# A hybrid decoder block on one core: 28 of its 64 input blocks moved into a Strassen stage, and its attention summed by parts

## The chip, the core and the metric

The kernel runs on one core of a Trainium2 chip as one launch. The metric is device time in microseconds from start to end of the launch, the median over several runs. Work is spread over five engines that run their own instruction lists in order and wait for each other through semaphores: TensorE (PE: matrix products and transpositions, results in PSUM), VectorE (DVE), ScalarE (ACT), GpSimd (POOL) and SyncE (SP: it issues most transfers). A profile is one execution traced by the hardware; rows name an engine, a line of the kernel, and tiles as `out<-in`. "PEld" is PE's load of the stationary operand, which overlaps the products.

## The reference

One decoder layer over 1024 positions of width 1024, with 16 learned tokens put in front (1040 positions in all). All arithmetic is in float32.

```python
h = concat([meta, x])                       # (1040, 1024)
xn = rms_norm(h, g_pre_mix)
b_c, c_c, h_c, q, k, v, g_conv, g_attn = split(xn @ w_in)   # eight parts, 1024 wide each
y_conv = b_c * causal_dwconv(c_c * h_c, conv_w_mix)         # 3 taps
o = stick_breaking_attention(q, k, v)                       # 16 heads of 64
merged = sigmoid(g_conv + b0) * (y_conv @ w_proj_conv) \
       + sigmoid(g_attn + b1) * (o @ w_proj_attn)
h = h + rms_norm(merged @ w_out, g_post_mix)
u, g = split(rms_norm(h, g_pre_ffn) @ w_up_gate)            # 2816 wide each
h = h + rms_norm((gelu(causal_dwconv(u, conv_w_ffn)) * g) @ w_down, g_post_ffn)
return h[16:]
```

The attention has no softmax. With z = q·k/8, f = sigmoid(-z) and S(t,s) the product of f(t,j) over all j with s <= j < t (and S = 1 from s = t on), the weight of key s for query t is A(t,s) = sigmoid(z(t,s)) · S(t,s+1), and zero from s = t on.

## The kernel before

Every float32 product is made of three products of rounded operands ("float32r"): each operand is split into a high part (a cast on ACT) and a low part (a subtraction); high·high, high·low and low·high are summed in PSUM. The helper `split` (lines 64 to 66) does it: line 65 is the ACT cast, line 66 the subtraction, on DVE or POOL by its last argument. So rows with L65 and L66 come from many places, and their tiles tell which.

The activations stand transposed, features on the 128 partitions and positions along the free axis: `xnT` holds the normalised input as 2 (high, low) x 8 feature blocks x 1040 positions. The 8192 columns of `w_in` are 64 blocks of 128. `Dense` (lines 81 to 158) works them off as a list of items; an item is one block: its weights are loaded (512 KB), split (line 110 on ACT, line 113 in four pieces on POOL), and multiplied with `xnT` in three column chunks of 342 to 356 positions, 24 matmuls each (lines 129 to 131): 72 matmuls per block. One `step()` is three matmuls. After a chunk the item's own `evac` takes the sums out of PSUM: for a q block two ACT casts, two DVE casts and two DVE subtractions (lines 229 to 231), for a k block an ACT cast and a DVE subtraction per head (242, 243), for a gate a sigmoid on ACT (304), for the convolution's three blocks a copy (278), a product on DVE (282), three taps (202 to 204) and another product (289).

Eight head pairs follow each other. The list holds, per pair, the v, q and k blocks of the next pair, three convolution blocks and one gate; the last pair has four gates, and five gates are left for the time behind the attention. The first three items are made while the input is still being normalised (`start_items`, `x_block`, lines 418 to 472).

The attention of a head is cut in nine query blocks of 114, in three units of three. `stage1` (lines 316 to 356) makes, per query block, z in chunks (lines 330, 331), f and sigmoid(z) on ACT (332, 333), and, one chunk later, S by a scan on DVE (340), then the product of sigmoid(z) with S shifted by one on POOL (346) and a triangular mask on POOL (348). The tile `fl` holds f and then S; `be` holds sigmoid(z) and then A. `stage2` (lines 358 to 398) transposes A by PE into PSUM tiles `tp` of two buffers (377), splits them (`ah` by ACT line 65, `al` by DVE line 66), and multiplies them with the values (367, 368); a product is issued two key blocks after its transpositions. The last two steps (394, 395) add the halves and write `ot`.

The loop at lines 506 to 536 merges three streams by written costs: stage 1 leads stage 2 by at least 2500 cost units, by at most two units of three blocks, and dense steps are dealt out so that a pair's share of the list ends with the pair's stage 1. The framework then places each engine's instructions; the order stands fixed in the built program.

Behind the attention come the two projections (items `pc` and `pa`), the output projection, and the feed-forward part. Its up-projection already uses Strassen's scheme in Winograd's form (`prep_pair`, `products`, lines 816 to 892): a pair of 128-column blocks is multiplied by seven half-size products instead of eight, each 4 x 3 matmuls on 256 to 512 columns. Weight combinations (`A11`, `S1`, ... tiles `a_op`) are split with the low part on POOL; token combinations (`T1` to `T4`) are made by DVE; three partial sums are copied out of PSUM by ACT (`snap`) and added at the end by DVE (918, 930). For an "u" pair each set of seven products is run twice, on 258 and on 256 columns; for a gate pair once on 512.

## Time and profile before

| | |
|---|---|
| median of 3 runs | 2027.19 us (2023.95 to 2030.04) |
| profiled execution, its own time | 2019.99 us |
| its span, first to last instruction | 2018.2 us |
| PE busy | 1968.4 us, 98% of the span |
| DVE, ACT, POOL busy | 1006.3, 853.3, 1022.7 us |
| mean granted TensorE clock | 0.993 |

How to read it: shares of busy time are means over stages. A row of a group gives busy microseconds, mean nanoseconds of one instruction, and the idle time of the engine in front of it with what ended it. PE's matmuls overlap, so the time of one row is longer than the distance from one start to the next; the distance is what counts. The input stage runs from 0 to about 67 us, the attention with its dense filling to about 925 us, the rest of the mixer to about 1300 us, the feed-forward part to the end.

### The profile page before, as it was taken

To read this page: it belongs to the slowest core of one execution; us is meant where nothing else is said; L and a number is where in the kernel's file an instruction comes from. 1 tells how busy PE (TensorE), PEld (TensorE's weight loads), DVE (VectorE), ACT (ScalarE), POOL (GpSimd) and SP (SyncE) were. 2 spreads that over 40 slices of the span, in tenths; PEclk is the share of its full clock that TensorE was granted. 3 is DMA by queue.
4 is the path that set the end of the run, shared out by engine and by line. 5 is a ranking of instruction groups with operands and counts; after the bars stand their busy time and mean duration, and the time that the engine had idled before them with its cause. 6 is when DMAs were issued, how large, how long until landed. Compare 5 with 4: busy or idle time off the path is not lost.

```text
span 2018.2 us, 30990 instructions
## 1 busy us (share of the span) xinstructions
PE 1968.4 (98%) x12228; PEld 1857.0 (92%) x12228; DVE 1006.3 (50%) x1545; ACT 853.3 (42%) x1771; POOL 1022.7 (51%) x1062
## 2 busy tenths in 40 slices
...
GB/s 137 43 63 43 53 32 64 43 53 43 42 53 43 58 39 62 32 64 73 189 221 156 188 214 114 97 31 126 63 84 67 102 66 82 92 174 111 84 84 136
DMA packets 56174, 177.58 MB, mean 88 GB/s; under 512 B 12872, under 2 KB 12872, under 8 KB 56028
## 3 DMA queue, kind: packets, MB, share of 16 engines
...
## 4 chain that ended last, share of the span: by engine, by line
PE 87%; DVE 7%; ACT 2%; DMA 2%; POOL 1%; issue 1%; ACTq 0%; DVEq 0%; SPq 0%; POOLq 0%
PE mm L129 14%; PE mm L130 14%; PE mm L131 14%; PE st L863 7%; PE st L867 7%; PE st L865 7%; PE tp L377 3%; PE st L1157 3%; PE st L1155 3%; PE st L1156 3%; PE av L368 2%; PE av L367 2%; PE z L331 2%; PE z L330 2%; PE po L706 1%; PE po L708 1%
## 5 line engine op out<-in xcount | busy, mean ns | idle before, releaser
L129 PE MATMUL mm<-xnT,whi 128*128 128x342 f32 (+2 forms) x1536 | 505.5, 329 | 0.3 <-ACT xnT L65 0.2
L130 PE MATMUL mm<-xnT,whi 128*128 128x342 f32 (+2 forms) x1536 | 494.0, 322 | 0.5 <-DVE xnT L66 0.5
L131 PE MATMUL mm<-xnT,wlo 128*128 128x342 f32 (+2 forms) x1536 | 492.3, 320 | 0.0
L346 POOL TENSOR_TENSOR be<-be,fl 114x271 f32<-114x271 f32 (+14 forms) x288 | 206.0, 736 | 310.3 <-DVE fl L340 301.6
L113 POOL TENSOR_TENSOR wlo<-raw,whi 128x256 fp32r<-128x256 f32 x320 | 254.8, 828 | 208.2 <-ACT whi L110 207.3
L130 PEld LDWEIGHTS mm<-xnT,whi 128*128 128x128 f32 x1536 | 291.0, 189 | 2.1 <-DVE xnT L66 1.0
L129 PEld LDWEIGHTS mm<-xnT,whi 128*128 128x128 f32 x1536 | 290.2, 189 | 2.9 <-ACT xnT L65 0.8
L131 PEld LDWEIGHTS mm<-xnT,wlo 128*128 128x128 f32 x1536 | 290.0, 189 | 0.0
L340 DVE TENSOR_TENSOR_SCAN fl<-fl,upper 114x128 f32<-114x128 f32 (+2 forms) x144 | 214.4, 1490 | 112.2 <-ACT fl L332 64.0
L66 POOL TENSOR_TENSOR a_op<-raw,a_op 128x512 fp32r<-128x512 f32 (+1 forms) x136 | 193.7, 1437 | 87.9 <-ACT a_op L65 85.6
L66 DVE TENSOR_TENSOR al<-tp,ah 114x342 fp32r<-114x342 f32 (+3 forms) x288 | 128.3, 452 | 148.8 <-ACT ah L65 147.5
L65 ACT CAST ah<-tp 114x342 fp32r<-114x342 f32 (+3 forms) x288 | 113.0, 398 | 165.3 <-PE tp L377 157.0
L863 PE MATMUL st<-opT,a_op 128*128 128x258 f32 (+2 forms) x528 | 172.3, 326 | 3.2 <-ACT snap L878 1.8
L865 PE MATMUL st<-opT,a_op 128*128 128x258 f32 (+2 forms) x528 | 170.1, 322 | 2.6 <-DVE opT L66 1.7
L867 PE MATMUL st<-opT,a_op 128*128 128x258 f32 (+2 forms) x528 | 170.0, 322 | 0.0
L332 ACT ACTIVATE fl<-z 114x348 f32<-114x348 f32 (+10 forms) x240 | 111.4, 464 | 123.6 <-PE z L331 93.5
L65 ACT CAST a_op<-raw 128x512 fp32r<-128x512 f32 (+1 forms) x136 | 85.1, 634 | 156.0 <-DMA raw<-in_w_up_gate_dram 51.8
L1162 DVE TENSOR_TENSOR acc<-acc,st 128x512 f32<-128x512 f32 x144 | 98.5, 687 | 91.1 <-PE st L1157 91.1
L865 PE MATMUL st<-opB,a_op 128*128 128x512 f32 (+2 forms) x396 | 127.6, 322 | 0.0
L863 PE MATMUL st<-opB,a_op 128*128 128x512 f32 (+2 forms) x396 | 127.6, 322 | 0.0
L867 PE MATMUL st<-opB,a_op 128*128 128x512 f32 (+2 forms) x396 | 127.2, 321 | 0.0
L377 PE MATMUL tp<-ident,be 114*114 114x114 f32 (+1 forms) x720 | 118.5, 262 | 4.1 <-DVE al L66 3.4
(168 smaller groups left out, 4320.5 us busy)
## 6 DMA issues: line engine op xcount, KB each, us to landing
raw<-in_w_in_dram SPq DMA_DIRECT2D x64, 512.0 KB, 3.3
raw<-in_w_up_gate_dram SPq DMA_DIRECT2D x44, 512.0 KB, 3.3
act_d<-owork SPq DMA_DIRECT2D x22, 512.0 KB, 4.3
araw<-act_d SPq DMA_DIRECT2D x22, 512.0 KB
raw<-in_w_down_dram SPq DMA_DIRECT2D x22, 512.0 KB, 3.3
...
```

The lines of the kernel that those rows point to most:

```text
L65: nc.scalar.copy(hi, src)
L66: (lo_engine or nc.vector).tensor_tensor(lo, src, hi.bitcast(F32), op=ALU.subtract)
L113: nc.gpsimd.tensor_tensor(lo[:, c], raw[:, c], hi[:, c].bitcast(F32), op=ALU.subtract)
L129: nc.tensor.matmul(ps, wh, xh, start=(kb == 0), stop=False)
L130: nc.tensor.matmul(ps, wh, xl, start=False, stop=False)
L131: nc.tensor.matmul(ps, wl, xh, start=False, stop=(kb == KB - 1))
L340: nc.vector.tensor_tensor_scan(fl[:, :nk][:, ::-1], fl[:, :nk][:, ::-1], upper[:, NT - nk:][:, ::-1], 1.0, op0=ALU.mult, op1=ALU.max)
L346: nc.gpsimd.tensor_tensor(be[:, a:e], be[:, a:e], fl[:, a + 1:e + 1], op=ALU.mult)
L377: nc.tensor.transpose(tp[:n, QB * j:QB * (j + 1)], blocks[j][0][:, k0:k0 + n], ident[:QB, :QB])
L863: nc.tensor.matmul(ps, wt[:, 0, k], xh, start=start and kb == 0, stop=False, skip_group_check=True)
L865: nc.tensor.matmul(ps, wt[:, 0, k], xl, start=False, stop=False, skip_group_check=True)
L867: nc.tensor.matmul(ps, wt[:, 1, k], xh, start=False, stop=stop and kb == 3, skip_group_check=True)
```

## The change

Three things change together, all ahead of the projections.

**A Strassen stage.** Of the 64 input blocks, 28 leave the list: the convolution's three blocks for seven of its eight column blocks, six attention gates and one convolution gate. They are taken in 14 pairs by the same seven-product scheme as the up-projection, each set of seven products run twice on 260 positions. The two halves of a pair are two 128-column blocks; the two token halves are positions 0 to 519 and 520 to 1039, so that B11, B21 and B22 are read straight from `xnT`, and only T1 to T4 are made, by `token_ops`: per feature block one addition on DVE, one on POOL (high plus low part), four subtractions on DVE and four splits (cast on ACT, low part on DVE). The stage stands behind five plain blocks (the first convolution's three and two gates), during which the token operands are made, and ahead of all attention. The weight combinations (`weight_ops`) are those of lines 829 to 850, with the low part on POOL as there, made for the next pair during a pair. The results go to tiles `su`; what follows on them (product of two blocks, three taps, product with the third, sigmoid, store) is put in a list `todo`, and one entry is taken after each of the first six products of a set.

**A shorter list beside the attention.** The list keeps 36 blocks: the five, 24 of v, q and k, and seven gates, three of them with the last pair and four behind the attention.

**Attention by parts.** Since A(t,s) = S(t,s+1) - S(t,s), the sum of A·v over s is v at the block's last position plus the sum of S(t,s)·(v(s-1) - v(s)). So the values are differenced once per pair (`dv`, DVE), the sigmoid of +z, the products on POOL and the mask go away, stage 2 transposes `fl` itself, and one addition on POOL per pair puts the block-end values back (`VE`). `fl` gets a buffer name per block size (two buffers for the six smaller, one for the three larger), and stage 1 may lead by three units instead of two.

The cut diff (a line of `...` marks what is left out):

```diff
             V[p] = vv
+            ends = VE[p] = heads.tile([P, 9], F32, name="ve", tag="ve", bufs=2)
+            nc.gpsimd.tensor_copy(ends, vt[:, P - 1:NT:QB])
+            dv = work.tile([P, NT], F32, name="dv", tag="wk", bufs=4)
+            nc.vector.tensor_tensor(dv[:, 1:], vt[:, :NT - 1], vt[:, 1:], op=ALU.subtract)
+            nc.scalar.mul(dv[:, 0:1], vt[:, 0:1], -1.0)
...
-                    nc.tensor.transpose(tp[:m, k * P:(k + 1) * P], vt[:, s0:s0 + m], ident)
+                    nc.tensor.transpose(tp[:m, k * P:(k + 1) * P], dv[:, s0:s0 + m], ident)
...
             nk = P + QB * b
             q0 = QB * b
-            fl = work.tile([P, NT], F32, name="fl", tag="fl")[:QB]
-            be = work.tile([P, NT], F32, name="be", tag="be", bufs=6)[:QB]
+            fl = work.tile([P, nk], F32, name="fl", tag=f"fl{b}", bufs=2 if b < 6 else 1)[:QB]
...
                 nc.scalar.activation(fl[:, c0:c0 + n], z, AF.Sigmoid, scale=-0.125)
-                nc.scalar.activation(be[:, c0:c0 + n], z, AF.Sigmoid, scale=0.125)
                 c0 += n
                 if late:
                     late.pop(0)()
                 if c0 < nk:
                     yield n
-            def weights(fl=fl, be=be, nk=nk):
-                nc.vector.tensor_tensor_scan(fl[:, :nk][:, ::-1], fl[:, :nk][:, ::-1],
-                                             upper[:, NT - nk:][:, ::-1], 1.0,
+            def weights(fl=fl, nk=nk):
+                nc.vector.tensor_tensor_scan(fl[:, ::-1], fl[:, ::-1], upper[:, NT - nk:][:, ::-1], 1.0,
                                              op0=ALU.mult, op1=ALU.max)
-                w = -(-(nk - 1) // (-(-nk // 384)))
-                for a in range(0, nk - 1, w):
-                    e = min(a + w, nk - 1)
-                    nc.gpsimd.tensor_tensor(be[:, a:e], be[:, a:e], fl[:, a + 1:e + 1],
-                                            op=ALU.mult)
-                nc.gpsimd.affine_select(out=be[:, nk - QB:nk], in_=be[:, nk - QB:nk],
-                                        pattern=[[-1, QB]], compare_op=ALU.is_gt, fill=0.0,
-                                        base=0, channel_multiplier=1)
 
             late.append(weights)
-            res.append((be, nk))
+            res.append((fl, nk))
...
         if (h, g) == (1, 2):
+            ov = ot[:, :NQ].rearrange("p (b n) -> p b n", n=QB)
+            nc.gpsimd.tensor_tensor(ov, ov, VE[p].unsqueeze(2).to_broadcast([P, 9, QB]), op=ALU.add)
             nc.sync.dma_start(o_d[p * P:(p + 1) * P, :], ot[:, :NQ])
...
-    gate_items = [item_gate(1, ob) for ob in range(8)] + [item_gate(0, ob) for ob in range(8)]
-    n_gate = [1, 1, 1, 1, 1, 1, 1, 4]
-    items, marks = [], []
+    n_gate = [0] * 7 + [3]
+    std_gates = [item_gate(0, ob) for ob in range(1, 8)]
+    gp["p"], gp["n"] = sring, 6
+    items, marks = items_conv(0) + [item_gate(1, 0), item_gate(1, 1)], []
+    n_early = len(items)
     items += [item_v(0), item_q(0), item_k(0)]
     gi = 0
     for p in range(NPAIR):
-        items += items_conv(p)
         for _ in range(n_gate[p]):
-            items.append(gate_items[gi])
+            items.append(std_gates[gi])
             gi += 1
         if p + 1 < NPAIR:
             items += [item_v(p + 1), item_q(p + 1), item_k(p + 1)]
         marks.append(len(items))
-    items += gate_items[gi:]
+    items += std_gates[gi:]
     n_gates = len(items)
-    dense = Dense(ps_mm, items)
+    dense = Dense(ps_mm0, items)
+    dense.stop = n_early
+
+    tops = {}
+    HT = NT // 2
+
+    def token_ops():
+        for kb in range(4):
+            a, b = wk_tile("xa"), wk_tile("xb")
+            nc.vector.tensor_tensor(a, xnT[:, 0, kb].bitcast(F32), xnT[:, 1, kb].bitcast(F32), op=ALU.add)
+            nc.gpsimd.tensor_tensor(b, xnT[:, 0, kb + 4].bitcast(F32), xnT[:, 1, kb + 4].bitcast(F32),
+                                    op=ALU.add)
+            e1, o1, e2, o2 = a[:, :HT], a[:, HT:], b[:, :HT], b[:, HT:]
+            sub(nc.vector, o1, o1, e1)
+            split_top("T1", kb, o1)
+            sub(nc.vector, o1, o2, o1)
+            split_top("T2", kb, o1)
+            sub(nc.vector, e1, o1, e1)
+            split_top("T3", kb, e1)
+            sub(nc.vector, e2, e2, o1)
+            split_top("T4", kb, e2)
+            yield
...
+        start_chunk = start_items(x_block)
+
+    t_ctx = ctx.enter_context(ExitStack())
+    tpool = t_ctx.enter_context(pool("tpool"))
+    for name in ("T1", "T2", "T3", "T4"):
+        tops[name] = tpool.tile([P, 2, 4, HT], F32R, name=f"t{name}")
+    tops_gen = token_ops()
+
+    for i in range(2):
+        next(tops_gen)
+        start_chunk(i, 9)
     dense.i, dense.total = 2, 48
-    dense.until(3)
+
+    RING1 = ["ap", "ap", "ap", "ap", "wlo", "whi", "wlo", "whi"]
...
+    def strassen(a_of, moving, n, bank, snaps, evac):
+        def mm(ps, a, b, start, stop):
+            wt = a_of[a]
+            for kb in range(4):
+                k = slice(kb * P, (kb + 1) * P)
+                xh, xl = moving(b, kb)
+                nc.tensor.matmul(ps, wt[:, 0, k], xh, start=start and kb == 0, stop=False,
+                                 skip_group_check=True)
+                nc.tensor.matmul(ps, wt[:, 0, k], xl, start=False, stop=False,
+                                 skip_group_check=True)
+                nc.tensor.matmul(ps, wt[:, 1, k], xh, start=False, stop=stop and kb == 3,
+                                 skip_group_check=True)
+
+        s = [snaps[k][:, :n] for k in range(3)]
+        b1, b3 = bank()[:, :n], bank()[:, :n]
+        mm(b1, "A11", "B11", True, True)
+        nc.scalar.copy(s[0], b1)
+        yield
+        mm(b3, "S1", "T1", True, True)
+        nc.scalar.copy(s[1], b3)
...
+        mm(b1, "A22", "T4", False, True)
+        evac(1, 0, b1, None)
...
+    def done_ch(cb):
+        if ("c", cb) in mixed and ("h", cb) in mixed:
+            c, y = mixed.pop(("c", cb)), mixed.pop(("h", cb))
+            mixed["y", cb] = y
+            todo.append(lambda: nc.gpsimd.tensor_tensor(c, c, y, op=ALU.mult))
+            todo.append(lambda: None)
+            todo.append(lambda: conv3(y[:, :NQ], c[:, T0 - 2:], NQ, lambda k: w_mix(k, cb)))
+
...
+    def done_gate(which):
+        def done(ob, u):
+            g = u[:, T0:]
+
+            def finish():
+                nc.scalar.activation(g, g, AF.Sigmoid, bias=bias_gate(which, ob))
+                nc.sync.dma_start((gc_d, ga_d)[which][ob * P:(ob + 1) * P, :], g)
+            todo.append(finish)
+        return done
+
...
+    early_blocks = []
+    for cbs in ((1, 2), (3, 4), (5, 6)):
+        for base, done in ((8, done_c), (16, done_h), (0, done_b)):
+            early_blocks += blocks_of(base, done, cbs)
+    early_blocks += blocks_of(8, done_c, [7]) + blocks_of(16, done_h, [7]) + blocks_of(0, done_b, [7])
+    early_blocks += blocks_of(56, done_gate(1), range(2, 8)) + blocks_of(48, done_gate(0), [0])
+    early_pairs = [early_blocks[k:k + 2] for k in range(0, len(early_blocks), 2)]
+
...
+    def prep_early(i):
+        got = early_ops[i] = {}
+        yield from weight_ops(*early_raw.pop(i), got, ring1_tile, tmp_e)
+        load_early(i + 1)
+
...
+    prep = prep_early(0)
+    for k in range(3 * (n_early - 2)):
+        dense.chunk()
+        next(tops_gen, None)
+        if k == 3:
+            load_early(0)
+        elif k > 3:
+            next(prep, None)
+    dense.until(n_early)
+    for _ in prep:
+        pass
+    ps0.close()
...
+    for i in range(len(early_pairs)):
+        last = i + 1 == len(early_pairs)
+        prep = iter(()) if last else prep_early(i + 1)
+        if last:
+            dense.stop = None
+            dense.load(n_early)
+        tiles = [wk_tile("su") for _ in range(2)]
+        for si in range(2):
+            n = HT // 2
+            j0 = si * n
+
+            def moving(name, kb, j0=j0, n=n):
+                return token_op(name, kb, j0, n)
+
+            for k, _ in enumerate(strassen(early_ops[i], moving, n, bank_s, snaps_e,
+                                           early_evac(i, tiles, j0, n))):
+                if (7 * si + k) % 2:
+                    next(prep, None)
+                if k < 6 and todo:
+                    todo.pop(0)()
+                if last and (si, k) == (1, 2):
+                    dense.prep(n_early)
+        for _ in prep:
+            pass
+        early_ops.pop(i)
+    for fn in todo:
+        fn()
+    psS.close()
+    t_ctx.close()
+    early_ctx.close()
...
+    dense.until(n_early + 3)
...
-        if n1 >= len(ends1) or n1 >= n2 + 2:
+        if n1 >= len(ends1) or n1 >= n2 + 3:
```

How it moves instructions, at three places. First PE in the middle of the attention, at the z chunks (`z<-kk`) of a head's last unit, where the blocks of 926 and 1040 keys are made. Before, three dense steps stand between two chunks:

```order
L330 MATMUL z<-kk,qh 114x464
L331 MATMUL z<-kk,ql 114x464
L129 MATMUL mm<-xnT,whi 128x342
L130 MATMUL mm<-xnT,whi 128x342
L131 MATMUL mm<-xnT,wlo 128x342
L129 MATMUL mm<-xnT,whi 128x342
L130 MATMUL mm<-xnT,whi 128x342
L131 MATMUL mm<-xnT,wlo 128x342
L129 MATMUL mm<-xnT,whi 128x342
L130 MATMUL mm<-xnT,whi 128x342
L131 MATMUL mm<-xnT,wlo 128x342
L330 MATMUL z<-kk,qh 114x462
```

In the changed kernel one dense step stands there:

```order
L338 MATMUL z<-kk,qh 114x464
L339 MATMUL z<-kk,ql 114x464
L137 MATMUL mm<-xnT,whi 128x342
L138 MATMUL mm<-xnT,whi 128x342
L139 MATMUL mm<-xnT,wlo 128x342
L338 MATMUL z<-kk,qh 114x462
L339 MATMUL z<-kk,ql 114x462
L137 MATMUL mm<-xnT,whi 128x342
L138 MATMUL mm<-xnT,whi 128x342
L139 MATMUL mm<-xnT,wlo 128x342
L338 MATMUL z<-kk,qh 114x348
L339 MATMUL z<-kk,ql 114x348
```

What moved: two of three dense steps left each gap.

Second DVE at the same depth of the attention: scans (`fl<-fl,upper`) and low parts (`al`). Before, three scans stand ahead of a unit's nine low parts:

```order
L340 SCALAR_TENSOR_TENSOR fl<-fl,upper 114x128
L340 SCALAR_TENSOR_TENSOR fl<-fl,upper 114x242
L340 SCALAR_TENSOR_TENSOR fl<-fl,upper 114x356
L66 TENSOR_TENSOR al<-tp,ah 128x342
L66 TENSOR_TENSOR al<-tp,ah 114x342 x6
L66 TENSOR_TENSOR al<-tp,ah 114x228
L66 TENSOR_TENSOR al<-tp,ah 114x114
L395 TENSOR_TENSOR ot<-av,ot 64x342
L340 SCALAR_TENSOR_TENSOR fl<-fl,upper 114x470
```

In the changed kernel, in a stretch without evacuations:

```order
L347 SCALAR_TENSOR_TENSOR fl<-fl,upper 114x128
L347 SCALAR_TENSOR_TENSOR fl<-fl,upper 114x242
L347 SCALAR_TENSOR_TENSOR fl<-fl,upper 114x356
L347 SCALAR_TENSOR_TENSOR fl<-fl,upper 114x470
L347 SCALAR_TENSOR_TENSOR fl<-fl,upper 114x584
L347 SCALAR_TENSOR_TENSOR fl<-fl,upper 114x698
L66 TENSOR_TENSOR al<-tp,ah 128x342
L66 TENSOR_TENSOR al<-tp,ah 114x342 x6
L66 TENSOR_TENSOR al<-tp,ah 114x228
L66 TENSOR_TENSOR al<-tp,ah 114x114
L393 TENSOR_TENSOR ot<-av,ot 64x342
L347 SCALAR_TENSOR_TENSOR fl<-fl,upper 114x812
```

What moved: six scans in a row stand ahead of the nine low parts, where it was three.

Third PE in the new stage, where the product A11·B11 ends and S1·T1 (`tT_500`) begins. Each triple of lines 560, 562 and 564 stands four times per product; there is nothing between products:

```order
L560 MATMUL st<-xnT,s_op 128x260
L562 MATMUL st<-xnT,s_op 128x260
L564 MATMUL st<-xnT,s_op 128x260
L560 MATMUL st<-tT_500,s_op 128x260
L562 MATMUL st<-tT_500,s_op 128x260
L564 MATMUL st<-tT_500,s_op 128x260
```

What moved: 2352 such rows (14 pairs of 168) stand in one piece ahead of the first z, for 2016 rows of lines 129 to 131 that stood among the attention.

170 lines of the change are left out of this document (140 added, 30 removed).

## The prediction

> **What bounds the kernel now.** I read the page's shares first, then windows of the stages, then PE's waits.
>
> ```profile
> span 2018.2 us, 30990 instructions
> PE 1968.4 (98%) x12228; PEld 1857.0 (92%) x12228; DVE 1006.3 (50%) x1545; ACT 853.3 (42%) x1771; POOL 1022.7 (51%) x1062
> PE 87%; DVE 7%; ACT 2%; DMA 2%; POOL 1%; issue 1%; ACTq 0%; DVEq 0%; SPq 0%; POOLq 0%
> ```
>
> PE is busy for all but 50 us and carries 87% of the chain that ended last. The windows (columns: stretch, its length, busy time and count of PE, PEld, DVE, ACT, POOL, granted clock, DMA) say whether that holds where the change is made:
>
> ```profile
> 0.00:42.00 42.00, 26.19 (x150) 24.16 (x151) 29.89 (x75) 24.80 (x51) 11.18 (x19) 1.00 0.46 165
> 259.10:370.18 111.08, 110.97 (x737) 108.57 (x736) 61.02 (x90) 58.39 (x135) 65.16 (x85) 1.00 0.14 48
> 1050.00:1150.00 100.00, 100.00 (x641) 100.00 (x640) 15.40 (x35) 14.51 (x21) 42.40 (x51) 1.00 0.58 173
> 1450.00:1600.00 150.00, 150.00 (x947) 134.94 (x946) 68.69 (x85) 64.49 (x111) 84.87 (x63) 1.00 0.21 72
> ```
>
> The second is one head pair of the attention, from one scan of 698 keys to the next pair's. PE lacks 0.11 of 111.08 us there; DVE works 61.02 us, 55%. PE is the bound, with much room under it. The first window is the input stage, where PE waits for normalised rows. PE's waits in the whole run:
>
> ```profile
> PE tp L184 <- DVE xn L462: 14.9, 3, 9.1
> PE tp L377 <- DVE al L66: 3.4, 5, 2.1
> ```
>
> The first belongs to the input stage. The second is all that PE loses to the attention's transposition buffers: 3.4 us in 16 heads, 0.21 us a head.
>
> **The matmuls saved.** In the third window only 342-column matmuls run: 641 in 100 us, 0.156 us each. Two plain blocks are 144 of them (a few of 344): 144 x 0.156 = 22.5 us. A pair in the new stage is 7 x 4 x 3 x 2 = 168 matmuls of 260 columns. The nearest row is the up-projection's 258-column matmul; first and last of sixteen in a row:
>
> ```profile
> 1404.25 0.28 PE L863 MATMUL st<-opB,a_op 128*128 128x258 f32 x1
> ...
> 1406.06 0.28 PE L863 MATMUL st<-opT,a_op 128*128 128x258 f32 x1
> ```
>
> Fifteen distances in 1.81 us are 0.1207 us, for 260 columns 0.1216; 168 x 0.1216 = 20.4 us. That saves 2.05 us a pair, **29 us** for 14 pairs. That the scheme saves an eighth of the products is so; the narrower matmul gives part back, since 0.1216 us for 260 columns is dearer per column than 0.156 for 342.
>
> **The new stage's own losses.** Weight combinations, PSUM copies and low parts per pair are those of the up-projection's "u" pairs, and the fourth window shows these with PE full: by the distances above (and 0.233 for 512 columns, as 4.19 us hold 18 of them) 949 matmuls fit in 150 us, and 947 ran.
>
> ```profile
> 1399.84 0.39 PE L867 MATMUL st<-opB,a_op 128*128 128x512 f32 x1
> ...
> 1404.03 0.39 PE L867 MATMUL st<-opT,a_op 128*128 128x512 f32 x1
> ```
>
> The `todo` entries come on top, but DVE and POOL have half of that window free and PE has eight PSUM banks. Between 0.2% and 1% of 286 us is 0.6 to 3 us; I take **+2**.
>
> **Token operands T1 to T4.** They need all of `xnT`, which is complete about here (last transpositions, from the chain):
>
> ```profile
> 39.38 0.88 PE tp L184 x8
> ```
>
> Then PE has 18 steps of the first two items and three whole items, (54 + 216) x 0.156 = 42 us, before the second Strassen product needs T1. DVE has in that time 4 additions of 1040, 16 subtractions and 16 low parts of 520 columns. The rows:
>
> ```profile
> L775 DVE TENSOR_TENSOR xr<-xr 128x1032 f32<-128x1032 f32 (+3 forms) x9 | 16.7, 1856 | 0.1
> L775 DVE TENSOR_TENSOR raw<-raw 128x512 f32<-128x512 f32 x44 | 51.7, 1175 | 107.6 <-POOL a_op L66 106.6
> L775 DVE TENSOR_TENSOR raw<-tmp_s,raw 128x512 f32<-128x512 f32 x21 | 15.6, 744 | 3.2 <-POOL a_op L66 1.2
> L66 DVE TENSOR_TENSOR opT<-xr,opT 128x1032 fp32r<-128x1032 f32 (+3 forms) x8 | 12.6, 1589 | 0.1
> ```
>
> 4 x 1.86 + 16 x (0.74 to 1.18) + 16 x 0.80 = 32 to 39 us. The first convolution's evacuations and taps and the first weight combinations add about 9: 41 to 48 against 42. So PE waits 0 to 7 us at the new stage's door; I take **+3**. What covers this work is the five plain blocks; without them all of it would be seen.
>
> The two widths of like subtractions, 1175 and 744 ns, differ by what POOL does beside them. [...]
>
> **Handover to the attention.** The v block's tile lies where the last gates are stored from; that takes two sigmoids and a store.
>
> ```profile
> act_d<-owork SPq DMA_DIRECT2D x22, 512.0 KB, 4.3
> ```
>
> About 7 us, while three PSUM buffers hold three chunks of 24 x 0.156 = 3.7 us, 11 us. Nothing, or up to 4 if the store queues; **+1**.
>
> **The attention beside a shorter list.** Per pair four of seven blocks go: 4 x 72 x 0.156 = 44.9 us, so PE's 110.97 become 66.0. What leaves the other engines:
>
> ```profile
> L333 ACT ACTIVATE be<-z 114x348 f32<-114x348 f32 (+10 forms) x240 | 110.6, 461 | 0.0
> L346 POOL TENSOR_TENSOR be<-be,fl 114x271 f32<-114x271 f32 (+14 forms) x288 | 206.0, 736 | 310.3 <-DVE fl L340 301.6
> L348 POOL TENSOR_SCALAR_AFFINE_SELECT be<-be 114x114 f32<-114x114 f32 x144 | 113.6, 789 | 10.1
> ```
>
> ACT loses 110.6/8 = 14 us a pair beside the blocks' own work, POOL 40. None of it was on the path, so it gains nothing directly. DVE loses only the convolution's share:
>
> ```profile
> L289 DVE TENSOR_TENSOR yy<-yy,mm 128x342 f32<-128x342 f32 x24 | 12.0, 498 | 1.7 <-PE mm L131 1.7
> L203 DVE SCALAR_TENSOR_TENSOR yy<-cc,par,yy 128x1026 f32<-128x1026 f32 x8 | 10.7, 1339 | 11.8 <-ACT yy L202 11.8
> L204 DVE SCALAR_TENSOR_TENSOR yy<-cc,par,yy 128x1026 f32<-128x1026 f32 x8 | 11.1, 1385 | 0.0
> L282 DVE TENSOR_TENSOR cc<-cc,mm 128x342 f32<-128x342 f32 x16 | 8.2, 512 | 14.5 <-PE mm L131 14.5
> ```
>
> With 4.1 more for eight wider ones of L282, 46/8 = 5.8 us a pair; the differenced values cost one subtraction of 1040, 1.9. DVE: 61.0 - 5.8 + 1.9 = 57.1 of 66.0 us, 86% where it was 55%. PE stays the bound by sums, but DVE runs its list in order, and behind one of its scans wait low parts, behind these the transposition buffers, behind these PE:
>
> ```profile
> L340 DVE TENSOR_TENSOR_SCAN fl<-fl,upper 114x128 f32<-114x128 f32 (+2 forms) x144 | 214.4, 1490 | 112.2 <-ACT fl L332 64.0 <-issue 23.4 <-POOL be L346 21.5
> L340 DVE TENSOR_TENSOR_SCAN fl<-fl,upper 114x128 f32<-114x128 f32 x16 | 7.7, 481 | 16.4 <-ACT fl L332 16.4
> L340 DVE TENSOR_TENSOR_SCAN fl<-fl,upper 114x812 f32<-114x812 f32 x16 | 30.9, 1932 | 23.9 <-issue 14.4 <-ACT fl L332 9.6
> L340 DVE TENSOR_TENSOR_SCAN fl<-fl,upper 114x926 f32<-114x926 f32 x16 | 35.2, 2200 | 11.7 <-issue 9.0 <-ACT fl L332 2.4
> L340 DVE TENSOR_TENSOR_SCAN fl<-fl,upper 114x1040 f32<-114x1040 f32 x16 | 40.1, 2508 | 16.3 <-POOL be L346 9.7 <-ACT fl L332 6.5
> L340 DVE TENSOR_TENSOR_SCAN fl<-fl,upper x141: 424/1375/2853, 68.9 to 924.8; 114x128 f32<-114x128 f32 x16, 114x242 f32<-114x242 f32 x16, 114x356 f32<-114x356 f32 x16, 114x470 f32<-114x470 f32 x16
> ```
>
> Lower bound for PE's wait: today's 0.21 us a head, 3 us in all. Upper: two of the three long scans (mean 2.2 us) uncovered but for two products and a dense step, 5 x 0.156 = 0.8 us: 2 x 1.4 = 2.8 us a head, 45 in all. In between I let the wait grow as share over rest, my estimate: 0.55/0.45 = 1.2 becomes 0.86/0.14 = 6.1, five times, 17 us. If the scans, with POOL's products gone, all took 12% less (424 ns, the least, for a mean of 481 at 128 keys), DVE would have 54 us, 82%, and the factor would be 3.7: 12 us. I take **+14**.
>
> **Sum.** -29 + 2 + 3 + 1 + 14 = -9 us. The profiled execution took 2019.99 us (1.8 beside its span), 7 under the median of 2027.19; I put the difference on the median: **2018 us**. With all losses at their lower ends it is -29 + 1 + 0 + 0 + 3 = -25, 2002; with all at their upper ends -29 + 3 + 7 + 4 + 45 = +30, 2057.
>
> **Rivals.** *All losses hide:* 2002. For it speaks that DVE and PE are each below their sums and that stage 1 may now run three units ahead; against it that only one dense step is left between z chunks.
>
> *DVE's order becomes the bound, slower:* the place is a unit's start in stage 2, where long scans stand ahead of or between low parts. Price 2.8 us a head, 45 in all: -29 + 6 + 45 = +22, 2049. It decides from 1.4 us a head, (29 - 6)/16. For it speaks the 86%; against it that a scan's result is needed a unit later, so DVE may run late for a while.
>
> *The token operands are late:* if DVE and POOL hold each other up beyond the rows above, say 12 us in place of 3, the sum is 0: 2027.
>
> *The change doesn't do what it says:* the stage has 2352 matmuls where 2016 go, so this is excluded; only its size is open.
>
> **How the numbers follow.** Forecast 0.42, its own range 2006 to 2027; all hidden 0.25; DVE's order 0.20; late operands 0.13. 0.3% of the median is 6 us, about what a measurement tells from no change: faster means under 2021, slower over 2033. Faster: 0.29 of the forecast, 0.25, 0.02 = 0.56; same: 0.13 and 0.07 = 0.20; slower: 0.20 and 0.04 = 0.24. The range goes from just under the best sum to just under the slow rival's: 1999 to 2045.
>
> **What would show it.** Right: a new stage of about 288 us with PE full; 67 to 68 us between the scans of 698 keys of two pairs; PE's wait for `al` some 14 us in all; little wait for T1. A pair period of 66 us means all hidden, of 69 or more the slow rival. Wrong altogether it would be if PE's 260-column matmul were not 0.12 us apart, or if a load or a store, not DVE, held PE in the new stage.

## The result and the profile after

| | before | changed |
|---|---|---|
| median, us | 2027.10 (2023.95 to 2030.04) | 2086.39 (2084.05 to 2088.0) |
| ratio | | 1.0288, 95% interval 1.0272 to 1.0305 |
| span of the profiled execution, us | 2018.2 | 2083.5 |
| granted clock, mean | 0.993 | 0.986 |

The change is slower by 2.9%; 0.4% faster was forecast. The page of the changed kernel, its span, shares and chain by engine:

```profile
span 2083.5 us, 31488 instructions
PE 1973.4 (95%) x12564; PEld 1833.2 (88%) x12564; DVE 1110.3 (53%) x1694; ACT 836.4 (40%) x1702; POOL 811.9 (39%) x643
PE 56%; DVE 11%; DMA 7%; ACT 4%; POOL 4%; issue 4%; ACTq 0%; DVEq 0%; SPq 0%; POOLq 0%
```

PE has no less busy time than before (1968.4), although the stage saves 29 us of matmuls, and 110 us of the span without work where it was 50. PE carries 56% of the chain in place of 87%. Windows of the changed kernel (columns as in the prediction: stretch, length, busy time and count of PE, PEld, DVE, ACT, POOL, granted clock, DMA) say where:

```profile
50.00:75.40 25.40, 18.41 (x105) 17.56 (x103) 25.12 (x23) 9.03 (x14) 18.44 (x12) 0.92 0.12 42
75.40:80.00 4.60, 4.58 (x16) 4.58 (x17) 4.60 (x6) 1.90 (x4) 3.37 (x3) 0.50 0.01 4
97.10:409.90 312.80, 293.93 (x2354) 291.68 (x2353) 106.63 (x157) 109.44 (x220) 152.76 (x110) 0.96 0.24 72
609.82:682.73 72.91, 68.57 (x447) 62.86 (x447) 54.48 (x83) 40.16 (x94) 15.28 (x17) 1.00 0.09 30
1069.80:1165.30 95.50, 91.84 (x576) 90.04 (x576) 27.48 (x51) 20.93 (x38) 26.02 (x33) 1.00 0.62 201
1165.30:1260.30 95.00, 92.32 (x578) 91.73 (x577) 15.05 (x40) 18.93 (x33) 56.09 (x62) 0.98 0.69 192
```

In order: the plain blocks of the start (PE idle for 7 of 25 us, then 4.6 us at half clock), the whole new stage, one head pair of attention, and the two projections, which the kernel before did in

```profile
1014.20:1104.30 90.10, 90.10 (x577) 90.10 (x577) 26.56 (x47) 19.38 (x34) 26.40 (x33) 1.00 0.57 189
1104.30:1196.20 91.90, 90.57 (x578) 90.29 (x577) 15.30 (x40) 18.94 (x33) 57.04 (x62) 1.00 0.70 199
```

And PE's waits in the whole run of the changed kernel:

```profile
PE tp L375 <- DVE al L66: 21.4, 31, 1.0
PE st L560 <- ACT snap_e L570: 13.9, 4, 4.1
PE st L560 <- DVE su L666: 4.9, 6, 2.9
PE tp L269 <- DVE vv L66: 4.8, 7, 0.8
PE mm L137 <- DVE yy L298: 4.7, 1, 4.7
PE mm L137 <- DVE gal L876: 2.6, 1, 2.6
PE mm L137 <- DVE gcl L855: 2.6, 4, 0.9
PE z L338 <- ACT fl L340: 2.1, 7, 0.4
PE tp L269 <- DVE dv L262: 2.0, 6, 1.0
```

The last matmul that reads `xnT` (end of the gates) stands at 1069.5 us where it stood at 1014.0: +55.5. The prediction had -9 up to there. The pieces:

- **Start.** The stage begins at 97.1 us. By the prediction's own rows PE could have been there at 39.4 + 0.9 + 42 = 82, but those rows take the last transpositions but one for the last. The last of all, of the last 16 positions, ended at 43.5 us here; 264 of the 360 matmuls of 0.156 us were left then, which gives 84.7. That is +12.
- **New stage.** 312.8 us for what took 14 x 22.5 = 315 us in plain blocks: a gain of 2 instead of 29.
- **Attention with its handover.** What is left: 55.5 - 12.4 + 2 = +45. From the third on a pair takes 72.7 to 72.9 us, not 66.0. Counted from the stage's end at 410.0 us, 31 blocks of 11.23 us and eight pairs without their blocks (66.0 - 3 x 11.23 = 32.3 us each) would be through at 1016.5 us: 53 us are lost. The same rates put the kernel before 7 us too early, and the difference is the +45 again.
- **Behind.** The projections take 95.5 and 95.0 us, where they took 90.1 and 91.9: +8.5. All that follows is within 2 us.

### The profile page after: what moved, and what is told of

Its sections match the earlier page's. It is cut to its first block, busy times and chain, and to the rows that moved or that the text cites. A ratio compares the mean times of both kernels' runs of the same rounds, so it can differ in the third digit from the quotient of the medians.

```text
span 2083.5 us, 31488 instructions
## 1 busy us (share of the span) xinstructions
PE 1973.4 (95%) x12564; PEld 1833.2 (88%) x12564; DVE 1110.3 (53%) x1694; ACT 836.4 (40%) x1702; POOL 811.9 (39%) x643
## 4 chain that ended last, share of the span: by engine, by line
PE 56%; DVE 11%; DMA 7%; ACT 4%; POOL 4%; issue 4%; ACTq 0%; DVEq 0%; SPq 0%; POOLq 0%
PE st L1120 6%; PE st L1122 5%; PE st L1124 5%; PE mm L139 5%; PE mm L138 5%; PE mm L137 5%; PE st L1414 3%; PE st L1412 3%; PE st L1413 3%; DVE fl L347 3%; PE tp L375 3%; PE av L366 2%; DMA xv<-in_x_dram 2%; PE av L365 2%; POOL a_op L66 2%
## 5 line engine op out<-in xcount | busy, mean ns | idle before, releaser
L121 POOL TENSOR_TENSOR wlo<-raw,whi 128x256 fp32r<-128x256 f32 x208 | 177.9, 884 | 315.4 <-ACT whi L118 288.3
L137 PE MATMUL mm<-xnT,whi 128*128 128x342 f32 (+2 forms) x864 | 286.3, 332 | 6.5 <-DVE yy L298 4.7
L138 PE MATMUL mm<-xnT,whi 128*128 128x342 f32 (+2 forms) x864 | 279.9, 324 | 0.9 <-DVE xnT L66 0.9
L139 PE MATMUL mm<-xnT,wlo 128*128 128x342 f32 (+2 forms) x864 | 279.8, 324 | 0.6 <-POOL wlo L121 0.6
L66 POOL TENSOR_TENSOR a_op<-raw,a_op 128x512 fp32r<-128x512 f32 (+1 forms) x136 | 193.7, 1438 | 90.1 <-ACT a_op L65 87.6
L69 DVE TENSOR_TENSOR raw<-raw 128x512 f32<-128x512 f32 x72 | 72.1, 1001 | 209.9 <-POOL a_op L66 106.3
L137 PEld LDWEIGHTS mm<-xnT,whi 128*128 128x128 f32 x864 | 164.9, 191 | 9.1 <-DVE yy L298 5.0
L138 PEld LDWEIGHTS mm<-xnT,whi 128*128 128x128 f32 x864 | 164.9, 191 | 2.6 <-DVE xnT L66 1.4
L139 PEld LDWEIGHTS mm<-xnT,wlo 128*128 128x128 f32 x864 | 164.5, 190 | 0.9 <-POOL wlo L121 0.9
L66 DVE TENSOR_TENSOR al<-tp,ah 114x342 fp32r<-114x342 f32 (+3 forms) x288 | 122.4, 450 | 54.5 <-ACT ah L65 51.8
L65 ACT CAST a_op<-raw 128x512 fp32r<-128x512 f32 (+1 forms) x136 | 85.1, 634 | 159.2 <-DMA raw<-in_w_up_gate_dram 54.5
L560 PE MATMUL st<-tT,s_op 128*128 128x260 f32 x448 | 129.8, 290 | 18.9 <-ACT snap_e L570 13.9
L375 PE MATMUL tp<-ident,fl 114*114 114x114 f32 (+1 forms) x720 | 117.1, 266 | 22.3 <-DVE al L66 21.4
L66 POOL TENSOR_TENSOR s_op<-raw,s_op 128x512 fp32r<-128x512 f32 x84 | 118.7, 1426 | 42.4 <-ACT s_op L65 33.8
L1122 PE MATMUL st<-opB,a_op 128*128 128x512 f32 (+2 forms) x396 | 127.8, 323 | 1.8 <-DVE opB L66 1.8
```

The costliest lines, as they stand in the source:

```text
L65: nc.scalar.copy(hi, src)
L66: (lo_engine or nc.vector).tensor_tensor(lo, src, hi.bitcast(F32), op=ALU.subtract)
L121: nc.gpsimd.tensor_tensor(lo[:, c], raw[:, c], hi[:, c].bitcast(F32), op=ALU.subtract)
L137: nc.tensor.matmul(ps, wh, xh, start=(kb == 0), stop=False)
L138: nc.tensor.matmul(ps, wh, xl, start=False, stop=False)
L139: nc.tensor.matmul(ps, wl, xh, start=False, stop=(kb == KB - 1))
```

## The experiments

Where a run is read by stretch, the pair of attention is measured from one pair's subtraction `dv` to the next's, and the new stage from its first to its last matmul. The diffs show only the lines that matter, and their comments are this text's. "One run" is a single timed execution with its profile. The executions of the kernel before lie between 2017.7 and 2030.0 us, so a few microseconds between the totals of single runs mean nothing; a pair's period mostly repeats within 0.3 us inside a run.

### Each part alone

The first kernel is the kernel before with attention by parts, all else as before (seven equal `fl` buffers):

```diff
-            nc.scalar.activation(be[:, c0:c0 + n], z, AF.Sigmoid, scale=0.125)
-            for a in range(0, nk - 1, w):          # be *= next fl, on GpSimd
+            nc.vector.tensor_tensor(dv[:, 1:], vt[:, :NT - 1], vt[:, 1:], op=ALU.subtract)
-            res.append((be, nk))
+            res.append((fl, nk))
```

> The kernel before with the attention by parts alone; the list of blocks beside the attention is as long as before, fl has seven equal buffers and stage 1 leads by at most two units. Theory (the loss in the attention comes from DVE's order with too little dense work between, not from the sum by parts): a head pair still takes 111 to 112 us, the total is within 8 us of the kernel before, 2019 to 2035. Rival (the sum by parts itself costs: the differenced values are late for the transposition of v, or the one addition on POOL holds the store): 2 us or more a pair, 2043 or more.

Measured: 2039.19 us, ratio 1.0081 (1.0062 to 1.0101); a pair 112.7 us for 111.1 before. From its waits:

```profile
PE tp L184 <- DVE v L73: 16.7, 1, 16.7
PE tp L268 <- DVE dv L261: 3.6, 7, 1.2
PE tp L371 <- DVE vv L66: 3.3, 6, 0.6
```

In between the theory and the rival: the sum by parts costs 1.6 us a pair beside the long list. PE's new waits stand at the value block, whose copy, subtraction and split it reaches too early. The first row lies in the input stage, whose rows have other buffers in this kernel than in the change: PE's first product on `xnT` begins 6 us later than before, and these are not the sum's.

The second is the changed kernel with the old attention (lead of two units):

> The changed kernel with the attention of the kernel before (sigmoid of +z, product and mask on POOL, lead of two units); stage and short list stay. Theory: the short list is what exposes DVE's order, so a pair takes 72 us or more, and with POOL's products beside the scans some us more: total 2080 to 2110. Rival (the sum by parts costs): clearly under the changed kernel, 2060 or less.

Measured: 2187.22 us, ratio 1.0817 (1.078 to 1.0854), a pair 86 to 89 us, PE waiting for `be`, `ah` and `al`. The theory's side, but far beyond its 2110: beside the short list the sum by parts, with the lead of three units that goes with it, is worth 100 us. Neither half of the change alone was faster than the kernel before.

### The start

DVE, POOL and PE in the changed kernel at 66 to 76 us:

```profile
66.74 0.69 DVE L69 TENSOR_TENSOR xb<-xb,xa 128x520 f32<-128x520 f32 x1
72.01 2.93 DVE L69 TENSOR_TENSOR xa<-xa 128x520 f32<-128x520 f32 x1
74.87 0.92 DVE L298 TENSOR_TENSOR yy<-yy,mm 128x342 f32<-128x342 f32 x2
```
```profile
70.97 3.42 POOL L431 TENSOR_TENSOR xb<-xnT 128x1040 f32<-128x1040 f32 x1 [1.78 <-DVE tT L66]
```
```profile
75.42 0.66 PE L137 MATMUL mm<-xnT,whi 128*128 128x342 f32 x1 [4.69 <-DVE yy L298]
```

A subtraction of 520 columns takes 0.69 us, and 2.9 us where POOL's 3.4 us sum of `xnT` runs: it ends 0.55 us after that sum does (three of the sixteen subtractions take as long, and end 0.55 to 0.57 us after such a sum). The plain b block's evacuation (L298) stands behind, and PE waits 4.7 us for it. The granted clock is 0.50 from 74.5 to 81.3 us, so the 6 us of work that follow take 3 us more. Earlier waits of 1.7 us for `whi` and 0.6 for `wlo` have a stretch of 3.4 us at 0.50 with them, from 54.1 us on: 1.7 us more. Together that is 11.7 of the 12.4 us. The kernel before shows the same: 44 of the 65 subtractions of 512 columns in the prediction's two rows of L775 began with no instruction of POOL running and took 0.68 to 0.69 us; the other 21 began while one ran, took 1.30 to 1.79 us, and ended 0.55 us after it.

The experiment puts two more gates into the start (seven plain blocks, 13 pairs) and moves the b block back:

```diff
-    items = items_conv(0) + [item_gate(1, 0), item_gate(1, 1)]
+    items = cv[:2] + [item_gate(1, 0), item_gate(1, 1), cv[2], item_gate(1, 2), item_gate(1, 3)]
-        next(tops_gen, None)
+        if k % 3 == 1:
+            next(tops_gen, None)
```

> The changed kernel, with two more attention gates as plain blocks ahead of the new stage (seven plain blocks, 13 pairs of products instead of 14), the plain b block two places later, and the token operands and weight operands spread over the longer time. By the matmuls alone it costs 22.5 - 20.4 = 2.1 us. Theory: the start loses 12-15 us since VectorE has token operands, taps and the b block's evacuation at once and is busy 10 of 10 us from 60 to 90 us; with 22 us more of plain blocks it is not: the stage begins at 108-112 us instead of 97.1 + 22.5 = 119.6, and the run is at 2076-2082 us. Rival: the start's loss is the weight operands' chain (ScalarE, GpSimd), which is as long whatever stands ahead: the stage begins at 117-121 us and the run is at 2086-2091 us.

Measured (one run): 2072.0 us, below the theory's 2076. The stage begins at 113.9 us, between theory (108 to 112) and rival (117 to 121): 5.7 us before the 119.6, and the wait for `yy` is gone with the half clock behind it. So VectorE's queue is the larger part of the start's +12, 4.7 + 3.0 us. What is left, 6 us, is the waits for `whi` and `wlo` with their half clock (4.0) and 1.0 us for a gate's evacuation at the stage's door; 1 us stays open.

### The new stage

One of three stalls of 4.1 us in the stage, on ACT and POOL of the changed kernel, with windows around it (a fourth of the kind takes 1.7 us):

```profile
211.06 1.16 ACT L203 ACTIVATE su<-su,par 128x1026 f32<-128x1026 f32 x1 [1.48 <-POOL su L606]
214.64 1.15 ACT L203 ACTIVATE su<-su,par 128x1026 f32<-128x1026 f32 x1 [2.42 <-POOL su L606]
215.69 0.35 ACT L570 COPY snap_e<-st 128x260 f32<-128x260 f32 x1
```
```profile
208.60 2.42 POOL L606 TENSOR_TENSOR su<-su 128x1040 f32<-128x1040 f32 x1
212.22 2.38 POOL L606 TENSOR_TENSOR su<-su 128x1040 f32<-128x1040 f32 x1
```
```profile
212.00:216.10 4.10, 0.04 (x1) 0.00 (x1) 3.73 (x2) 1.68 (x4) 2.60 (x2) 0.80 0.41 128
216.10:222.00 5.90, 5.90 (x29) 5.90 (x30) 4.82 (x5) 1.12 (x3) 1.54 (x1) 0.56 0.00 0
222.00:232.00 10.00, 10.00 (x86) 10.00 (x85) 2.66 (x5) 3.37 (x8) 3.57 (x3) 1.00 0.01 2
```

ACT waits 2.42 us for POOL's product c·y, to take the first tap; behind the tap, on the same queue, stands the copy of a PSUM sum to `snap_e`, for which PE waits. After 4.1 us without work PE runs 5.9 us at 0.56 of its clock: 29 matmuls where some 50 would fit. In the stage 18.9 us are idle (312.80 - 293.93) and 293.93 - 14 x 20.4 = 8 us are busy time beyond the sum; the mean clock of 0.96 fits them.

Four experiments took this apart. First the product on DVE:

```diff
-            todo.append(lambda: nc.gpsimd.tensor_tensor(c, c, y, op=ALU.mult))
+            todo.append(lambda: nc.vector.tensor_tensor(c, c, y, op=ALU.mult))
```

> The changed kernel with the product of two convolution blocks in the new stage on DVE instead of POOL. Theory (ACT's tap waits for POOL's product, and the PSUM copy that PE needs stands behind that tap on ACT; each stall of 4 us is followed by a stretch at half the granted clock): the waits for snap_e (13.9 us) go, the stage falls from 313 to 290 to 297 us, total 2065 to 2072. Rival (the stage is short of operands or loads): stage over 308 us, total 2080 or more.

Measured: 2071.61 us, ratio 1.0242 (1.0225 to 1.0259). The total is as expected, the stage is not: 304.5 us, between theory and rival. The waits for `snap_e` are gone, those for `su` rise from 4.9 to 12.8 us. About 5 us of the total came behind attention, in the projections.

Then the taps later:

```diff
-            todo.append(lambda: conv3(y[:, :NQ], c[:, T0 - 2:], NQ, lambda k: w_mix(k, cb)))
+            todo.extend([lambda: None] * 4)      # once both products of a pair are posted
+            for t in taps: todo.extend(conv_steps(*t))   # one tap to a step
```

> The changed kernel, with one thing moved: the two products c*y of a pair of c and h blocks are still GpSimd's, but the three taps of each stand four product steps later, one tap to a step, where the change put all three two steps behind the product. Theory: the new stage loses its time because ScalarE's first tap waits for GpSimd's product with the copy of a PSUM sum to snap_e queued behind it, 4 us each time, after which the granted clock falls: with the taps later the stage falls from 312.8 us to 288-295 us and the run to 2060-2070 us. Rival: the stage is short of VectorE or GpSimd time in the sum over it; then the stalls move to another place and the stage stays above 305 us, the run above 2077 us.

Measured (one run): 2084.13 us, waits for `snap_e` 13.9 us as before. Nothing had moved: in the order as built both first taps stood ahead of the same `snap_e` copy again, for the framework had not kept them where they were written. In the changed kernel's own order, too, the first taps of both blocks stand together: one per product step is how the finishing is written, not how it is issued. With the taps held behind what is written ahead of them (and other edits in the other stretches):

```diff
+        return [lambda: tc.keep_in_program_order(nc.scalar.activation(d, ...)),
+                lambda: tap(1), lambda: tap(0)]          # held in the same way
```

> The changed kernel with three edits, each read in its own stretch. Start: the two further plain gates of the run before. New stage: the taps four steps later, as tried before, but now held in the order in which they are written (before, the scheduler had put them ahead of the copy to snap_e again, so that nothing had moved on ScalarE). Attention: each scan is likewise kept behind what is written ahead of it on VectorE. Theory for the stage (ScalarE's taps stand ahead of the copies while GpSimd's product is late): the waits for snap_e go, and 13 pairs take 268-275 us (20.6-21.2 us each); rival (the sums on VectorE are the bound): above 282 us. Theory for attention (scans standing ahead of al): the pair falls from 72.8 to 69-71 us; rival (the order of the lumps of work on TensorE sets it): 72-73.5 us. Run by the theories 2028-2047 us, by the rivals above 2062 us.

Measured (one run): 2073.39 us. The `snap_e` waits are gone, but 13 pairs take 285.0 us, 21.9 each, the rival's number: the stalls are now `su`, up to 3.4 us. DVE of this kernel:

```profile
245.15 4.18 DVE L623 SCALAR_TENSOR_TENSOR su<-su,par 128x1026 f32<-128x1026 f32 x2
249.25 0.42 DVE L684 TENSOR_TENSOR su<-st,snap_e 128x260 f32<-128x260 f32 x1
```
```profile
249.72 0.39 PE L562 MATMUL st<-tT,s_op 128*128 128x260 f32 x1 [3.40 <-DVE su L684]
```

No single tap or product is the cause, then, but a tight place that each of them can hit. In `strassen` bank b1 is read by `evac(1, 1, b1, ...)` and written again by A22·T4; between stands one product, 12 x 0.12 or about 1.45 us, and the two taps take 4.18. With the taps two steps apart a pair still took 21.6 us (run g3 below). The last experiment widens the place: the halves of a pair's tokens alternate, product by product, each with its own snap buffers, so that three products lie between a sum's reading and its next writing (the expectation counted two).

```diff
-        for si in range(2):
-            for k, _ in enumerate(strassen(...)):
+        halves = [strassen(early_ops[i], moving, n, bank_s, snaps_e[si], ...) for si in range(2)]
+        for j in range(14):
+            next(halves[j % 2])
```

It was run with edits of attention (h1, expectation below). Its 13 pairs, and then for comparison the 13 of the run with the longer start, whose stage was otherwise the change's:

```profile
113.40:381.10 267.70, 262.83 (x2183) 261.61 (x2184) 116.49 (x147) 98.21 (x201) 142.56 (x98) 1.00 0.25 76
```
```profile
113.90:402.70 288.80, 271.18 (x2183) 269.27 (x2184) 102.26 (x147) 99.23 (x201) 139.99 (x98) 0.96 0.23 70
```

(The first is of h2, the same stage again.) 20.6 us a pair for 22.2, clock 1.00 for 0.96, and DVE is no less busy, with taps of up to 3.4 us. That settles the stage: not load, but one product of slack against a queue worked off in order, and the lower clock behind the long stalls. (The order and the second set of snap buffers came together; which of them alone would do, no run tells.)

### Attention

DVE and PE of the changed kernel at one stall:

```profile
621.53 2.31 DVE L347 TENSOR_TENSOR_SCAN fl<-fl,upper 114x1040 f32<-114x1040 f32 x1
623.76 0.91 DVE L66 TENSOR_TENSOR al<-tp,ah 114x342 fp32r<-114x342 f32 x2
```
```profile
623.17 0.32 PE L137 MATMUL mm<-xnT,whi 128*128 128x342 f32 x1
624.31 0.41 PE L375 MATMUL tp<-ident,fl 114*114 114x114 f32 x2 [0.82 <-DVE al L66]
```

A scan stands ahead of `al`, `al` frees a transposition buffer, PE waits for the buffer. 1.14 us lie between two starts that are 0.16 apart when nothing waits; the wait is shown as 0.82, since it counts from the modelled end. Counted by the period, a pair loses 72.8 - 66.0 = 6.8 us, where the rows of waits above (21.4 + 4.8 + 2.1 + 2.0 in 8 pairs) show 3.8.

How much of it are scans? This run leaves out the scan of the first half of each block's keys:

> The changed kernel with the scan left out for the first half of each query block's keys, so the weights of those keys are not the attention's; all else runs. Theory (PE waits because a low part stands behind a scan on DVE): scans are at most half as long, DVE loses about 12 us a pair, a pair falls from 72.8 to 67 to 69 us, total 2045 to 2058. Rival (the round trip PE, ACT, DVE, PE over two transposition buffers sets the pace): a pair stays at 71 us or more, total 2072 or more.

Measured (one run): 2054.67 us, a pair 69.6 to 69.9 us, the wait for `al` 6.0 us in place of 21.4. The total is the theory's, the pair just above it. Scans make 3.1 of the 6.8 us at least. The run can't say whether by their load or by where they stand. Single edits of the changed kernel for the other candidates, first e8, then e4:

```diff
-            dense.defer(1, lambda: tokens(0, 4, P))
+            dense.defer(8, lambda: tokens(0, 4, P))
...
-    ps_mm = psA.enter_context(pool("ps_mm", 3, space=PSUM))
+    ps_mm = psA.enter_context(pool("ps_mm", 2, space=PSUM))
-    ps_tp = psA.enter_context(pool("ps_tp", 2, space=PSUM))
+    ps_tp = psA.enter_context(pool("ps_tp", 3, space=PSUM))
```

> The changed kernel, with the transpositions of a pair's value differences dv put 8, 11 and 14 dense steps behind the end of the value block, where the change put them 1, 2 and 3 steps behind it. Theory: 1.65 us a pair is lost because TensorE's queue reaches these transpositions before ScalarE's copy, VectorE's subtraction and the split are through; later, they cost nothing: the pair falls from 72.8 to 70.8-71.5 us, the run to 2070-2079 us, and the waits of tp for dv and vv go. Rival: VectorE's order as a whole holds TensorE, and a wait that goes there comes back as a wait for al: the pair stays at 72.3-73 us, the run within 5 us of 2086 us.

> The changed kernel, with three PSUM buffers for transpositions and two for the dense blocks, where it has two and three. Theory (VectorE's order): scans of 1.6 to 2.3 us stand ahead of al, and one more buffer of 0.7 us of TensorE's work covers a part of each stall: the pair falls from 72.8 to 70.5-72 us, and the run to 2068-2080 us, unless the dense blocks' evacuation holds TensorE instead. Rival: the two transposition buffers are what set the pace, and VectorE's order does not matter: the pair falls to 66-68 us and the run to 2031-2048 us. Third: the dense blocks need their third buffer more, and the run is above 2090 us.

Measured (one run each): e8 2083.83 us, a pair 71.9 to 73.6; the waits for `dv` and `vv` (6.8 us) are gone, those for `al` are as large as before (14.8 and 7.3 at two places), and pair and run are the rival's. e4 2079.83 us, a pair 71.5: its theory by the numbers, and the wait moved to the product (`av` for `al`, 21.8). Scans held in order (f1, above): 72.6, the rival. With the third buffer in addition:

> The kernel of the run ahead of this one (start, taps and scans held in order) with three PSUM buffers for transpositions and two for dense blocks. By itself the third buffer moved the wait from the transposition to the product and brought 7 us in the run. Theory (what is left is jitter between TensorE and VectorE, which one more buffer evens out): 1-2 us a pair below the run ahead of this, 8-16 us in all. Rival: the wait only moves to the products again, within 0.5 us a pair of the run ahead, or worse for the dense blocks.

Measured (one run): 2075.79 us, a pair 72.0: 0.6 below f1, so nearest the rival. Then the order itself. The rule of stage 1 and 2 writes up to 12 steps of one kind in a row; the next two alternate them:

```diff
-        if n2 < len(ends1) and done1 < min(ends1[n2] + LAG, total1):
-            pick2 = False
+            at = ends1[n2] - u1 * min((ends2[n2] - done2) / u2, 1.0)
+            pick2 = done1 >= min(max(ends1[n2] + 800.0, at + 3200.0), total1)
```

> Start and taps as in the two runs ahead of this. In attention the order is written evenly: the rule that lets the sums of logits run ahead goes by the place within a unit, so that steps of the two halves alternate (one to three at a time), where the change writes lumps of up to 12 steps of one half; scans over 400 keys in two chained pieces; transpositions of dv later. Theory (VectorE has 57 us of work in 66, and only lumps make it late): the pair falls to 67-69 us, the run to 2012-2030 us. Rival (in an even order each scan stands ahead of an al that TensorE is about to want, and there is no stretch without them): the pair stays at 71-74 us, the run at 2045-2070 us.

> The even order of the run ahead of this with three PSUM buffers for transpositions and two for dense blocks. Theory: in the even order the wait for al is short each time, and one more buffer takes most of it: 1-2 us a pair below the run ahead, at 66-68 us a pair, the run at 2005-2022 us. Rival: within 0.5 us a pair of the run ahead.

Measured (one run each): 2087.57 and 2088.17 us, a pair mostly 75.4 and 74 to 76.5. The rivals' side, and worse than they had it: worse than the lumps. The two pieces of each scan stood side by side in the order as built, so that a low part behind them still waited for a whole scan.

Is it the list that is too short, or DVE that is too full? One gate a pair back into the list, at the expense of two pairs of the stage; and 4.4 us a pair off DVE (g1 is the first edit, g3 the second, g2 both):

```diff
-    n_gate = [0] * 7 + [3]
+    n_gate = [1] * 7 + [0]
...
-                nc.vector.tensor_copy(hi[other, c], ps[own])
+                nc.scalar.copy(hi[other, c], ps[own])
-            nc.vector.tensor_tensor(dv[:, 1:], vt[:, :NT - 1], vt[:, 1:], op=ALU.subtract)
+            nc.gpsimd.tensor_tensor(dv[:, 1:], vt[:, :NT - 1], vt[:, 1:], op=ALU.subtract)
```

> Of the 16 gate blocks four are plain ahead of the new stage, one is in it, seven stand in the list beside attention (one to a pair of heads, four blocks a pair instead of three) and four behind it; the new stage has 11 pairs of blocks. The taps are held in order and stand on steps of their own, none behind another. Theory (the list is too short to cover attention's waits): a pair with its gate takes 77.3-79 us (66.0 + 11.25 for the gate, and up to 1.7 of stalls), the run 2017-2030 us. Rival (the stalls are the same whatever the list): 82.5-84 us a pair and the run at 2055-2066 us. New stage: 20.5-21.0 us a pair if VectorE's row of taps was what held it, 21.9 if not.

> The run ahead of this with work taken off VectorE: the copy of q to the other half of the partitions goes to ScalarE (3.1 us a pair), the difference dv to GpSimd (1.3 us), and the transpositions of dv stand 8 to 14 steps later. Theory (list): within 1 us a pair of the run ahead, since one gate covers nearly all. Rival (VectorE's load): 2 us or more a pair below the run ahead.

> The changed kernel's list (no gate beside the first seven pairs), with the start of seven plain blocks, the spread taps, and the same 4.4 us a pair taken off VectorE. Theory (list): the pair falls by 1.7 us or less, to 71-72.7 us, and the run is at 2050-2062 us. Rival (VectorE's load, as in the run with half the scans, where 13 us a pair less load brought 3.1): 69-70.5 us, and the run below 2046 us.

Measured (one run each): g1 2081.61 us, a pair 84.0, which is 72.75 + 11.25: the gate covers nothing, the rival, with a total 15 us above it. Its stage takes 21.5 us a pair, near the 21.9 that was to mean that the row of taps was not it. g2 2084.44 us, a pair 82.9: 1.1 below g1, between theory and rival. g3 2070.94 us, a pair 73.1: neither, for a pair got no shorter at all. So one more block does not help, and 4.4 us less work on DVE brings 1.1 us or nothing. Only beside seven blocks a pair (e1) was the loss down to 1.6 us.

What was left as an explanation was that several limits hold at once: any one taken away, the next holds. The run with all of these edits, and the wide stage:

```diff
+            for j in range(np_):                 # two pieces over 500 keys
+                late.append(lambda j=j, piece=piece: piece(j))   # one to a step, held in order
```

> The changed kernel with: the start of seven plain blocks (13 pairs in the new stage); the two halves of a pair's tokens alternating product by product in the new stage, with a set of snap buffers each; in attention the even order (a step of logits to one or two steps of products), scans of over 500 keys in two pieces that are held in the written order so that al stands between them, three transposition buffers, and the copy of q to the other half of the partitions on ScalarE, dv on GpSimd, its transpositions later. Theory for the new stage (the row behind a PSUM sum is read by VectorE only 1.45 us, one product, before the sum is written again, and any tap of 1.3-2.9 us in front stalls TensorE): with 2.9 us between, 20.4-20.8 us a pair, 265-271 us in all; rival (VectorE's load as such): 279 us or more. Theory for attention (bursts of scans, and a transposition buffer freed only by al, both at once): 66-68 us a pair; rival (even order is worse by itself, as the two runs with it): 72-75.5 us a pair. Run: 1998-2018 us by the theories, where the kernel before takes 2018-2023 us; 2055-2070 us if only the stage's holds.

Measured: 2027.61 us, ratio 1.0027 (1.0015 to 1.0039); the stage 267.7 us, a pair 67.5 to 69.2 us, on the mean 68.5. (This kernel leaves out the last pieces of the last head's scans, some 2 us of DVE's work.) Both by the theories, attention half a microsecond above, and the run 10 us above theirs: the projections still waited. One long stall is left in a pair, 1.97 us between starts; DVE, POOL and PE there:

```profile
571.80 0.82 DVE L66 TENSOR_TENSOR al<-tp,ah 128x342 fp32r<-128x342 f32 x2
572.54 2.63 DVE L354 TENSOR_TENSOR_SCAN fl<-fl,upper 114x406 f32<-114x406 f32 x1
575.10 0.24 DVE L66 TENSOR_TENSOR al<-tp,ah 114x114 fp32r<-114x114 f32 x1
```
```profile
572.40 1.91 POOL L262 TENSOR_TENSOR dv<-vt 128x1039 f32<-128x1039 f32 x1
```
```profile
575.40 0.46 PE L374 MATMUL av<-al,vv 114*128 114x114 f32 x1 [1.81 <-DVE al L66]
```

406 keys take 1.0 us alone; here 2.63, begun 0.14 us after POOL's subtraction and ended 0.9 us after it, as in the start. That subtraction is `dv`, moved to POOL to relieve DVE. The stall also decides between the two lengths of a pair. Of the six pairs with this stall four had the half clock behind it, as in the first row, and two had not:

```profile
575.40:578.40 3.00, 3.00 (x11) 2.94 (x12) 1.54 (x2) 0.90 (x2) 0.98 (x2) 0.50 0.33 90
644.40:647.80 3.40, 3.40 (x25) 3.35 (x26) 2.23 (x4) 2.20 (x6) 0.97 (x2) 1.00 0.41 143
```

The pairs that began with the half clock took 69.0 to 69.2 us, those without 67.5 to 67.6. So in this run an idle stretch of 1.8 us cost some 1.4 us of clock on top in four of six cases.

The next run mends behind attention (six PSUM buffers for dense blocks):

```diff
+    psA.close()
+    dense.ps = psA.enter_context(pool("ps_mm3", 6, space=PSUM))
-            nc.gpsimd.tensor_tensor(ov, ov, VE[p]...)
+            nc.vector.tensor_tensor(ov, ov, VE[p]...)
```

> The run ahead of this (even halves, even order, three transposition buffers, held scan pieces) with: six PSUM buffers for the dense blocks once attention is over, in place of two; the addition of the last values to ot on VectorE instead of GpSimd; transpositions of dv 12 to 20 steps later; and a scan that is always written before the first transposition that reads it (in the run ahead of this the last head's last pieces were left out, some 2 us of VectorE). Theory: waits for gt, gcl and gal behind attention (3.1, 1.6 and 4.7 us) go, attention falls by 0.5-1 us a pair, and the run is at 2005-2016 us, ratio to the kernel before 0.993-0.998. Rival: with the waits for PSUM gone the projections wait for the loads of gates at the same places, and the stall at the scan beside GpSimd stays: 2020-2028 us, ratio 0.999-1.003.

Measured: **2013.92 us, ratio 0.9952 (0.9933 to 0.9971)**, beside 2022.73 of the kernel before: by the theory, and 0.5% faster than the kernel before. PE's waits for `gt`, `gcl` and `gal` in the projections are gone, and these take 90.2 and 91.5 us; the pair stays at 68.2 on the mean, so that part of the expectation failed and the stall beside POOL stays:

```profile
PE 1945.0 (97%) x12540; PEld 1835.2 (91%) x12540; DVE 1111.7 (55%) x1716; ACT 846.4 (42%) x1741; POOL 805.4 (40%) x644
PE av L383 <- DVE al L66: 11.9, 9, 1.8
PE st L578 <- ACT snap_e L594: 2.8, 3, 1.0
```

Last, the same with the lumps back:

> The run ahead of this with the change's own rule for the order of logits and products in attention (lumps of up to 12 steps of one kind), all else as there: three transposition buffers, scan pieces held in order, the copy of q on ScalarE and dv on GpSimd. Theory (bursts of scans are what stalls, and they come of the lumps): the pair goes from 68.2 back to 71 us or more, the run to 2035 us or more. Rival (buffer, pieces and VectorE's load did it, the order matters little): within 1 us a pair of 68.2, and the run at 2010-2022 us.

Measured (one run): 2033.98 us, a pair 70.7. Between the two, nearer to the theory: the lumps cost 2.5 us a pair, and buffer, held scans and DVE's relief together 2.0 (72.7 to 70.7), though singly they brought 1.2, 0.1 and nothing (the scans there were held whole, here in two pieces).

## Why the prediction was wrong, step by step

**Matmuls saved, -29: right.** First and last of 57 matmuls in a row in the changed kernel's stage:

```profile
204.72 0.28 PE L560 MATMUL st<-tT,s_op 128*128 128x260 f32 x1
...
211.40 0.28 PE L564 MATMUL st<-tT,s_op 128*128 128x260 f32 x1
```

That is 0.1193 us from start to start, where 0.1216 was taken. With the wide place a pair takes 20.6 us against the 20.4 worked out, for 22.5 in plain blocks.

**The new stage's own losses, +2 (0.6 to 3): the step that failed outright.** Measured +27 (312.8 - 14 x 20.4). The loss was read off the up-projection's "u" pairs, with PE full, and the finishing work was let pass because DVE and POOL "have half of that window free". Free time on the mean was the wrong measure. What counts is the 1.45 us between a PSUM sum's reading and its next writing, against single instructions of 1.2 to 3.5 us that finish a block. The up-projection has such taps too, but they run beside a gate pair's products of 512 columns. A tap of the kernel before, and PE's products from 1464 us on:

```profile
1464.90 1.54 DVE L203 SCALAR_TENSOR_TENSOR owork<-owork,par_ffn 128x1024 f32<-128x1024 f32 x1 [1.22 <-ACT owork L202]
L863 PE MATMUL st<-opB,a_op x4: 388/394/403, 1464.4 to 1466.5; 128*128 128x512 f32 x4
```

There one product is 12 x 0.233 = 2.8 us, so the same tap has room. The analogy took the width from the "u" pairs and the finishing work's harmlessness from the gate pairs; no run tested it. No end of the range knew the tight place. The text also named no clock: of the 27 us, some 8 are the lower clock behind stalls.

**Token operands, +3 (0 to 7): too small, +12 measured.** The mechanism was named by the two widths of like subtractions, and the rival of late operands had +12. But PE did not wait for T1 at the stage's door. It waited for a plain block's evacuation, which stood behind the token operands on DVE, and then ran at half clock; more plain blocks took 5.7 us away. One error was to price the subtractions by means (744 and 1175 ns): beside POOL's sum of `xnT`, which the change adds at that very place, one takes 2.9 us. Another was the row for the last transpositions, which were those of the last 16 positions, 4.4 us later:

```profile
43.79 0.66 PE L184 MATMUL tp<-ident,xn 16*128 16x16 f32 x8
```

**Handover, +1: not seen as a wait of its own** in the rows above; it is in attention's sum.

**Attention beside a shorter list, +14 (3 to 45): mechanism right, size wrong.** Scans ahead of `al`, `al` ahead of the transposition buffers, as the text had it, but +45 against the kernel before and 53 counted by rates, at the upper end of the range or over it. The estimate by "share over rest" (0.86/0.14) had no ground: DVE was busy for 54.5 of 72.9 us, 75%, when PE stalled. The place decides, not the share. The rival *DVE's order becomes the bound* had the mechanism and the price of 2.8 us a head, where 3.4 was measured by the pair period; its 2049 lacks the stage, the start's rest and the projections. Its word that DVE may run late for a while, given against it, reckoned with the scans' results but not with what stood behind them on DVE.

**Not foreseen at all:** the projections, +8.5. With three PSUM buffers for dense blocks they wait for evacuations that wait for the gates' loads, and part of the time runs at the lower clock (0.98 on the mean in the second); with six they take 90.2 and 91.5 us. The size is not steady: in the other runs with the short list and two or three buffers the two take 183.6 to 194.8 us together, here 190.5, before 182.0. Why three were enough before, no run tells; the list had five gates in front of them and has four.

**What would show it** was of use: PE not full in the stage, and 72.8 us for a pair where 69 or more was to mean the slow rival.
